# A two-layer streaming encoder: the sample's result turned in the value product's bank, and a rearranged start of layer A

## The chip, the cores and the metric

The kernel runs on one core of a Trainium2 chip. The metric is the device time of one execution in microseconds (us). Five engines work side by side, each through its own instruction list in order: TensorE (PE) multiplies and transposes, ScalarE (ACT) and VectorE (DVE) work on what PE leaves in its result banks, GpSimd (POOL) works on buffers, and SyncE (SP) issues every DMA transfer of this kernel. They wait for one another through semaphores.

## The reference: what is computed

Two layers, one after the other, over a prompt of 2048 tokens and a sample of 64 tokens that has caches of earlier keys and values. Cut to what matters:

```
def project(x, norm_g, w_in, q_g, k_g, n_heads, n_kv):
    h = rms_norm(x, norm_g)
    p = h @ w_in
...
    q, k, v, gate = jnp.split(p, [wq, wq + wkv, wq + 2 * wkv], axis=-1)
...
    q = rms_norm(q.reshape(*lead, n_heads, HEAD_DIM), q_g)
    k = rms_norm(k.reshape(*lead, n_kv, HEAD_DIM), k_g)
...
    op = prompt_band_attention(qp, kp, vp, past_chunks, bias_fn, sinks)
    y_p = x_p + (op * jax.nn.silu(gp)) @ w_out
...
    os_, nk, nv = sample_band_attention(qs, ks, vs, ck, cv, bias_fn, sinks)
    y_s = x_s + (os_ * jax.nn.silu(gs)) @ w_out
```

The model width is 1024, with 16 heads of 64. Layer A (index 0) has two key/value heads and a window of two earlier chunks of 64 tokens; layer B has 16 key/value heads and eight earlier chunks. The outputs are both results and the newest keys and values of both layers.

## The kernel before

**Precision.** Every fp32 operand is split into a high and a low part (`split_to`, line 579, and the casts in `load_act.split`): ScalarE casts the high part, DVE or POOL subtracts it from the source for the low part. A product is then three matmuls: high weight by high x, low weight by high x, high weight by low x (lines 477 to 479 in `project`).

**Units and passes.** The prompt is cut into eight units of 256 tokens (two tiles of 128); the sample is a ninth unit of 64. The order of the units is 0 to 6, the sample, 7. Layer A runs four passes `qd` over the units, each with four query heads; the first pass also projects k and v. Layer B runs eight passes `hp`, each with one pair of heads. At the end of a layer come output projections (`output_jobs`, lines 1366 to 1371).

**What sets the order.** PE's order is written out by hand: attention steps are emitted one by one, and `Filler` puts projection matmuls between them up to a mark. On the other engines a scheduler sets the order from the order of the code, the buffers and its own estimate of times. `Background` collects small steps (splits, low parts) and hands them out between attention steps; `behind` adds a dependency that only fixes an order on an engine.

**Result banks.** PE's results go to banks named by tags: `pj` (projections, two banks), `tp` (transpositions of queries, keys and gates, one bank), `o` (value products, one bank), and for scores and probabilities `sa` in layer A (four) or `sb` in layer B (two pairs). A step that takes a tag waits until the earlier user of that bank has been read.

**Layer B, one item.** For each unit of a head pair: `queries` transposes q and k into `tp`, ScalarE takes the high parts out (L1095, L1096) and DVE the low parts (L1100, L1104). `scores` multiplies (L1146, L1147), DVE adds the bias and takes the minimum (L1150), ScalarE takes the exponential (L1154), POOL forms the gate product G (L1168). `values` transposes the probabilities into `sb` (L609, five tiles at a time) and splits them into the tiles `ph` and `pl` (L581, L582), of which each has six slots for key tiles. `outputs` multiplies with the values in bank `o` (L1242, L1243). For the sample unit, `sample_outputs` multiplies in bank `o`, ScalarE and DVE add up the pieces (L1209, L1211), POOL multiplies by the gate (L1212), and `sample_turned` transposes this result into `tp`, from where ScalarE copies it out in two halves (L1219) for the store. The sample's turn occurs once in each head pair, eight times in all. As the sample unit is the last but one, the turn comes when `queries` for the next head pair's first unit has just filled `tp`.

**Bias tiles.** `bias_tile` loads the bias of a head into `BT` (L188) and POOL overwrites a corner (L189, L191). The bias vectors get to the form in which they are read over a copy: `spread` loads a row to all partitions (L170) and stores it skewed (L171). `spread_first` does it for the first four heads at once, through a tile that it borrows from `ph` (L197, L202).

**The start of layer A.** `load_act` loads x of a unit in four pieces into raw buffers `xraw` (L368; three buffers, `XB`), casts each (L382 on ScalarE, L383 on POOL) and, for the first two units, squares them (`square`). From the sums come the token scales (`token_scales`, `sums_to_scales`: two small matmuls L429, DVE, a power on POOL L434). For later units `row_scales` loads rows of x again into `xraw` (L451), ScalarE squares with a running sum (L453), POOL adds (L458) and raises to the power (L460). `first` projects unit 0, `gen` every other unit; `take_kv` and `take_qg` evacuate a projection, where ScalarE multiplies with the scale (L500). After unit 0, `first` also calls `token_scales` for unit 1.

Of the kernel before, what the change touches and what calls it, by code (L numbers as in the profile page):

```python
# [15 lines left out]
P = 128  # L16
# [5 lines left out]
UT = 256  # L22
# [11 lines left out]
XB = 3  # L34
# [16 lines left out]
def hybrid_encoder_kernel(  # L51
# [142 lines left out]
    def spread_first():  # L194
        row = t("ph", [P, 6, 256], 2, F32R).bitcast(F32).rearrange("p a b -> p (a b)")[:, : 4 * VL]
        src = vec[0, 0]
        ld = load(  # L197
            row.rearrange("p (h v) -> p h v", v=VL),
            bass.AP(tensor=src.tensor, offset=src.offset, ap=[[0, P], [VL, 4], [1, VL]]),
        )  # L200
        behind(ld.ins, held["w"])
        store(skew[0, 0:4].rearrange("h p v -> p h v"), row.rearrange("p (h v) -> p h v", v=VL))  # L202
        b = BT[:, 0:1024].rearrange("p (h k) -> p h k", h=4)
        src = skew[0, 0, 0, 127:128]
        load(b, bass.AP(tensor=src.tensor, offset=src.offset, ap=[[VL - 1, P], [P * VL, 4], [1, 256]]))
        nc.gpsimd.memset(b[0:64, :, 192:256], BIG)
        nc.gpsimd.memset(b[64:128, :, 0:64], BIG)
        return [b[:, h] for h in range(4)]
# [139 lines left out]
    def load_act(src, o, T, squares=False, joint=False, lead=None, cache=None, cached=False):  # L348
# [22 lines left out]
        def split(c):  # L371
            def fn():
                if len(raws) <= c:
                    bg.run(x.squares[c - XB])
                rv = raws[c]
                xx = t("xx", [P, 4 * OT], XN, F32R)
                xh, xl = parts = parts_of(xx, T, joint)
                if joint:
                    nc.scalar.copy(xh[:, :, :T], rv)
                    nc.gpsimd.tensor_tensor(xh[:, :, T:], rv, xh[:, :, :T].bitcast(F32), op=ALU.subtract)  # L380
                else:
                    nc.scalar.copy(xh, rv)  # L382
                    nc.gpsimd.tensor_tensor(xl, rv, xh.bitcast(F32), op=ALU.subtract)  # L383
                x.parts.append(parts)
                if cache is not None:
                    store(kept(c), xx[:, : 4 * T].bitcast(F32))
                if not squares:
                    fetch()
            return fn

        def square(c):
            def fn():
                s2 = t("res", [P, 2 * OT], 2)[:, : 2 * T].rearrange("p (k s) -> p k s", k=2)
                sq = nc.scalar.activation(s2, raws[c], AF.Square)
                if lead is not None and c > 0:
                    behind(sq.ins, held["wh"])
                part = t("o1" if x.sum else "G", [P, 256])
# [88 lines left out]
    def evacuate(layer, tt, n, ps, C, G, b=None):  # L486
# [11 lines left out]
        for dst, src in pieces:  # L498
            if n == P:
                nc.scalar.activation(dst, src, AF.Identity, scale=sc)  # L500
            else:
                nc.scalar.activation(dst[:n], src[n:], AF.Identity, scale=sc[n:])
# [173 lines left out]
    def layer_a():  # L676
# [4 lines left out]
        def add_unit(qd, place, unit):  # L681
# [59 lines left out]
            def first():  # L741
# [13 lines left out]
                for it, o in zip(mine, qgs):  # L755
                    take_qg(it, o[0])
                st.bias[0] = spread_first()
                token_scales(units[1], st.x[0, 1], psum("o", 512, 1))
                yield 2 * 3 * 512 / 2400

            def gen():
# [8 lines left out]
                for it in mine:  # L770
                    if qd == 0 and not heads_up:
                        out = []
                        c = yield from project(it.tile, xc, st.wkv, 256, out)
                        take_kv(it, out[0])
# [149 lines left out]
        def values(it):  # L924
            qd = it.qd
            tt, t0, n = it.tile
            ph = t("ph", [P, 6, 256], 2, F32R)
            pl = t("pl", [P, 6, 256], 2, F32R)
# [77 lines left out]
    def layer_b():  # L1006
# [168 lines left out]
        def values(it, i, h):  # L1175
            u, T, tiles = it.unit
            tt, t0, n = tiles[i]
            if i == 0:
                it.ph[h] = t("ph", [P, 6, 256], 2, F32R)
                it.pl[h] = t("pl", [P, 6, 256], 2, F32R)  # L1180
# [7 lines left out]
            for c in range(m):  # L1188
                transpose(PTv[:, c, :n], it.p[i, h][:n, c * P : (c + 1) * P])
            bg.anchor(*split_to(  # L1190
                it.ph[h][:, kb : kb + m, t0 : t0 + n], it.pl[h][:, kb : kb + m, t0 : t0 + n], PTv[:, :m, :n]
            ))
# [21 lines left out]
        def sample_turned(it):  # L1214
            tp = psum("tp", 512, 1)
# [7 lines left out]
        def outputs(it, h):  # L1223
# [15 lines left out]
            mm.append((VT[:, tb, h], tb - it.base, P, UT))  # L1239
# [272 lines left out]
```

## Time and profile before

| | us |
|---|---|
| median of three runs | 2322.2 |
| the three runs | 2326.36, 2320.93, 2322.2 |
| the profiled execution | 2330.51 |
| its span, first to last instruction | 2328.7 |
| PE busy in the span | 2259.3 |
| mean granted clock of PE | 0.991 |

A page of the profile gives the busy time of each engine, and groups of instructions by line. `L609` is line 609 of the kernel; where a helper records an operation, the line is the helper's (every transposition is L609), and the buffers tell what it is. `tp<-ident,o` is an instruction that writes `tp` and reads `ident` and `o`. In a timeline the first two columns are the start and the duration of an instruction, both in us; in brackets stands the idle time just ahead of it and what ended that. In a list of waits the columns are the total in us, the count and the longest. SPq is SP's list of DMA issues; the time there is that of the issue, not of the transfer. `DMA to landing` gives the time from issue to arrival for the transfers of one line.

### The profile page before, as it was taken

Reading aid. Unit: us, or ns where it says so; the run is one execution under the profiler, and the core shown is the slowest. Engines: PE = TensorE matmul, PEld = TensorE weight load, DVE = VectorE, ACT = ScalarE, POOL = GpSimd, SP = SyncE. Lnnn points to the kernel's source line nnn. Section 1 sums busy time; section 2 is a strip of 40 time slices with the busy share of each in tenths; the row PEclk is TensorE's granted clock in tenths of the full one; section 3 lists DMA queues with packets and bytes.
Section 4 is the critical chain, followed back from the end, with each engine's and each line's share of the span. In section 5 each row is a group of like instructions: output and inputs, shape, how many; then the busy total and the mean of one; then the engine's idle time right before and its main releaser. Section 6 shows DMA issues by size and latency. Waiting matters only on the chain.

```text
span 2328.7 us, 42202 instructions
## 1 busy us (share of the span) xinstructions
PE 2259.3 (97%) x13869; PEld 1984.3 (85%) x13869; DVE 1559.2 (67%) x5194; ACT 1432.8 (62%) x3632; POOL 839.5 (36%) x1196
## 2 busy tenths in 40 slices
PE   7899999999999999999999999999999999999999
PEld 6787888888889998888888888888888888888999
DVE  6779888887784446776767757667667577576211
ACT  6778877777773336765656656656556566565321
POOL 5554533333354556432222222222223222224443
PEclk9999999999999999999999999999999999999999
DMA  8846546754437767454543544544445435443665
GB/s 250 265 152 204 170 147 189 220 176 159 141 110 208 226 212 261 157 184 125 167 126 104 175 133 129 154 134 119 139 134 158 125 113 174 123 125 106 187 186 148
DMA packets 232124, 379.35 MB, mean 163 GB/s; under 512 B 24720, under 2 KB 163360, under 8 KB 231872
## 3 DMA queue, kind: packets, MB, share of 16 engines
q1 hardware_dynamic: 231904, 376.65, 52.7%
q8 instruction: 109, 1.79, 0.3%
q14 instruction: 111, 0.91, 0.1%
HBM read 296.13 MB, written 82.08 MB: 162 GB/s over the span
## 4 chain that ended last, share of the span: by engine, by line
PE 79%; DVE 8%; DMA 5%; ACT 4%; issue 2%; POOL 1%; SPq 1%; DVEq 0%; ACTq 0%; POOLq 0%
PE pj L477 13%; PE pj L479 12%; PE pj L478 12%; PE pj L1366 5%; PE pj L1367 5%; PE pj L1368 5%; PE sb L609 5%; PE o L1243 3%; PE o L1242 3%; PE tp L609 3%; PE sb L1147 3%; PE sb L1146 3%; DMA xraw<-in_x_rows_dram 2%; PE sa L609 2%; DVE pl L582 1%
## 5 line engine op out<-in xcount | busy, mean ns | idle before, releaser
L477 PE MATMUL pj<-wh,xx 128*128 128x512 f32 (+1 forms) x1648 | 671.0, 407 | 9.2 <-ACT pb L500 8.6
L479 PE MATMUL pj<-wh,xx 128*128 128x512 f32 (+1 forms) x1648 | 641.3, 389 | 0.0
L478 PE MATMUL pj<-wl,xx 128*128 128x512 f32 (+1 forms) x1648 | 638.7, 388 | 1.0 <-DVE wl L312 1.0
L479 PEld LDWEIGHTS pj<-wh,xx 128*128 128x128 f32 x1648 | 312.6, 190 | 68.3
L477 PEld LDWEIGHTS pj<-wh,xx 128*128 128x128 f32 x1648 | 314.1, 191 | 50.3 <-ACT pb L500 9.9
L478 PEld LDWEIGHTS pj<-wl,xx 128*128 128x128 f32 x1648 | 314.8, 191 | 40.0 <-DVE wl L312 1.4
L383 POOL TENSOR_TENSOR xx<-xraw,xx 128x528 fp32r<-128x528 f32 (+1 forms) x200 | 264.9, 1341 | 197.1 <-ACT xx L382 185.0
L540 POOL TENSOR_TENSOR f<-f,mhalf 128x4 f32<-128x4 f32 (+3 forms) x221 | 226.1, 1024 | 227.9 <-DVE f L536 219.0
L1154 ACT ACTIVATE p<-p,nm 128x640 f32<-128x640 f32 (+5 forms) x264 | 199.8, 757 | 175.2 <-DVE nm L1150 174.6
L1366 PE MATMUL pj<-xx,wh 128*128 128x264 f32 x1024 | 294.2, 287 | 1.2 <-DVE res L1371 1.0
L1367 PE MATMUL pj<-xx,wh 128*128 128x264 f32 x1024 | 291.7, 285 | 0.0
L1368 PE MATMUL pj<-xx,wl 128*128 128x264 f32 x1024 | 290.3, 283 | 0.0
L1150 DVE CUSTOM_DVE_ANT_0 p<-sb,BT 128x640 f32<-128x640 f32 (+5 forms) x272 | 196.8, 724 | 136.0 <-PE sb L1147 120.9
L582 DVE TENSOR_TENSOR pl<-sb,ph 128x640 fp32r<-128x640 f32 (+4 forms) x264 | 193.3, 732 | 117.0 <-ACT ph L581 114.2
L1002 POOL TENSOR_TENSOR o<-gt,o 128x256 f32<-128x256 f32 (+1 forms) x132 | 102.9, 779 | 386.1 <-DVE o L1001 122.8
L382 ACT CAST xx<-xraw 128x528 fp32r<-128x528 f32 (+1 forms) x200 | 122.2, 626 | 190.1 <-PE pj L1368 97.5
L581 ACT CAST ph<-sb 128x640 fp32r<-128x640 f32 (+4 forms) x264 | 163.5, 619 | 116.4 <-PE sb L609 111.1
L1366 PEld LDWEIGHTS pj<-xx,wh 128*128 128x128 f32 x1024 | 193.1, 189 | 2.1 <-DVE res L1371 1.6
L1367 PEld LDWEIGHTS pj<-xx,wh 128*128 128x128 f32 x1024 | 192.9, 188 | 0.2
L1368 PEld LDWEIGHTS pj<-xx,wl 128*128 128x128 f32 x1024 | 193.1, 189 | 0.0
L536 DVE CUSTOM_DVE_ANT_0 sq<-pa 128x64 f32<-128x64 f32 (+1 forms) x834 | 169.6, 256 | 30.8 <-ACT pa L500 28.8
L1371 DVE TENSOR_TENSOR res<-pj,res 128x264 f32<-128x264 f32 x128 | 55.0, 430 | 200.2 <-PE pj L1368 184.9
(210 smaller groups left out, 4788.6 us busy)
## 6 DMA issues: line engine op xcount, KB each, us to landing
xx<-xsb SPq DMA_DIRECT2D x224, 512.0 KB, 4.3
xx<-xsa SPq DMA_DIRECT2D x88, 512.0 KB, 4.8
xraw<-oga SPq DMA_DIRECT2D x64, 264.0 KB, 3.6
xraw<-ogb SPq DMA_DIRECT2D x64, 264.0 KB, 3.3
xsa<-xx SPq DMA_DIRECT2D x32, 512.0 KB, 4.5
wraw<-in_w_in_b_dram SPq DMA_DIRECT2D x64, 256.0 KB, 3.7
xsb<-xx SPq DMA_DIRECT2D x32, 512.0 KB, 4.0
xraw<-in_x_dram SPq DMA_DIRECT2D x40, 256.0 KB, 4.1
```

The source lines that it names most:

```text
L383: nc.gpsimd.tensor_tensor(xl, rv, xh.bitcast(F32), op=ALU.subtract)
L477: nc.tensor.matmul(ps[:n, :C], xh, wh, start=k == 0, stop=False)
L478: nc.tensor.matmul(ps[:n, :C], xh, wl, start=False, stop=False)
L479: nc.tensor.matmul(ps[:n, :C], xl, wh, start=False, stop=k == KC - 1)
L540: nc.gpsimd.tensor_tensor(fv, fv, mhalf[:n, :H], op=ALU.pow)
L582: b = nc.vector.tensor_tensor(dst_lo, src, dst_hi.bitcast(F32), op=ALU.subtract)
L609: nc.tensor.transpose(out, in_, ident[:n, :n])
L1150: mi = nc.vector.tensor_tensor_reduce(out=p[r, :nk], in0=S[r, o : o + nk], in1=b, op0=ALU.add, op1=ALU.min, scale=1.0, scalar=3e38, accum_ ...
L1154: ex = nc.scalar.activation(p[:n, :nk], p[:n, :nk], AF.Exp, scale=-1.0, bias=it.nm[:n, c : c + 1], accum_out=it.sm[:n, c : c + 1],)
L1366: nc.tensor.matmul(ps[:, :OT], wh, oh, start=k == 0, stop=False)
L1367: nc.tensor.matmul(ps[:, :OT], wh, ol, start=False, stop=False)
L1368: nc.tensor.matmul(ps[:, :OT], wl, oh, start=False, stop=k == KC - 1)
```

## The change

1. `sample_turned` takes bank `o` in place of `tp`.
2. There are four raw buffers for x in place of three (`XB`).
3. The tiles `ph` and `pl` have five key slots in place of six; in layer B the slot of a key tile is its index modulo five.
4. `spread_first` works in two halves of two heads each, since the borrowed tile is smaller: two loads and two stores in place of one each.
5. The casts of the third unit (the first without squares) are put behind the last square, and its second to fourth also behind the last evacuation of unit 0.
6. The token scales of unit 1 are computed in `gen` of unit 1, after its first k/v projection, and not at the end of `first`.

```
-XB = 3
+XB = 4
...
     def spread_first():
-        row = t("ph", [P, 6, 256], 2, F32R).bitcast(F32).rearrange("p a b -> p (a b)")[:, : 4 * VL]
...
-        store(skew[0, 0:4].rearrange("h p v -> p h v"), row.rearrange("p (h v) -> p h v", v=VL))
+        for h in (0, 2):
+            row = t("ph", [P, 5, 256], 2, F32R).bitcast(F32).rearrange("p a b -> p (a b)")
+            row = row[:, : 2 * VL].rearrange("p (h v) -> p h v", v=VL)
+            src = vec[0, h]
+            ld = load(row, bass.AP(tensor=src.tensor, offset=src.offset, ap=[[0, P], [VL, 2], [1, VL]]))
+            behind(ld.ins, held["w"])
+            store(skew[0, h : h + 2].rearrange("h p v -> p h v"), row)
...
+                if not squares and "first" in held:
+                    behind(cast.ins, held["square"])
+                    if c:
+                        behind(cast.ins, held["first"])
+                    if c == 3:
+                        held.pop("first")
...
+                held["square"] = sq.ins
...
-                nc.scalar.activation(dst, src, AF.Identity, scale=sc)
+                held["evac"] = nc.scalar.activation(dst, src, AF.Identity, scale=sc).ins
...
+                held["first"] = held["evac"]
                 st.bias[0] = spread_first()
-                token_scales(units[1], st.x[0, 1], psum("o", 512, 1))
...
                         c = yield from project(it.tile, xc, st.wkv, 256, out)
+                        if u == 1 and it is mine[0]:
+                            token_scales(unit, xc, psum("o", 512, 1))
                         take_kv(it, out[0])
...
-                transpose(PTv[:, c, :n], it.p[i, h][:n, c * P : (c + 1) * P])
+                transpose(PTv[:, (kb + c) % 5, :n], it.p[i, h][:n, c * P : (c + 1) * P])
...
         def sample_turned(it):
-            tp = psum("tp", 512, 1)
+            tp = psum("o", 512, 1)
             transpose(tp[0:HD, 0:P], it.o)
...
-            mm.append((VT[:, tb, h], tb - it.base, P, UT))
+            mm.append((VT[:, tb, h], (tb - it.base) % 5, P, UT))
```

Line numbers in the changed kernel are six to eight higher. The counts of instructions are the same on every engine, but for one load and one store more on SP. Three places of the order follow; a row gives the line, the operation and what it writes and reads.

PE at the second sample turn in layer B, before. `pj` is the projection of the next pass, `p` the probabilities, `o` in the fourth row the sample's result.

```order
L478 MATMUL pj_15645<-wl_14665,xx_15437 128x512
L479 MATMUL pj_15645<-wh_14664,xx_15437 128x512
L609 MATMUL sb_15652<-ident,p_15560 128x128 x5
L609 MATMUL tp_15666<-ident,o_3141_15590 64x128
L477 MATMUL pj_15645<-wh_14670,xx_15439 128x512
L478 MATMUL pj_15645<-wl_14671,xx_15439 128x512
```

The same place on PE after the change:

```order
L484 MATMUL pj_15648<-wl_14668,xx_15440 128x512
L485 MATMUL pj_15648<-wh_14667,xx_15440 128x512
L615 MATMUL sb_15655<-ident,p_15563 128x128 x5
L615 MATMUL o_15669<-ident,o_3142_15593 64x128
L483 MATMUL pj_15648<-wh_14673,xx_15442 128x512
L484 MATMUL pj_15648<-wl_14674,xx_15442 128x512
```

The turn keeps its place; only its bank is another, `o` for `tp`.

ACT in the head before, from the first k/v evacuation of unit 1 (`pa_545<-pj_520`). `res_481` is the first row scale, `KA`, `KB` and `VT` are keys and values.

```order
L500 ACTIVATE pa_545<-pj_520,rms_92 128x256
L816 ACTIVATE KA<-sa_559,ksc 64x128
L816 ACTIVATE KB<-sa_559,ksc 64x128
L560 CAST VT<-pa_545 128x2x64
L850 ACTIVATE q_133_574<-tp_571,qsc 64x2x128 x2
L500 ACTIVATE pa_596<-pj_555,rms_92 128x256
L500 ACTIVATE pb_597<-pj_555,rms_92 128x256
L453 ACTIVATE res_481,ms_478<-xraw_479 128x512
```

ACT there after the change, up to the same evacuation, now `pa_548<-pj_517`. The eight L459 are the row scales of units 2 and 3, the three L587 the casts of the cached keys and values.

```order
L459 ACTIVATE res_478,ms_475<-xraw_476 128x512
L459 ACTIVATE res_482,ms_475<-xraw_480 128x512
L459 ACTIVATE res_486,ms_475<-xraw_484 128x512
L459 ACTIVATE res_490,ms_475<-xraw_488 128x512
L459 ACTIVATE res_499,ms_496<-xraw_497 128x512
L459 ACTIVATE res_503,ms_496<-xraw_501 128x512
L459 ACTIVATE res_507,ms_496<-xraw_505 128x512
L459 ACTIVATE res_511,ms_496<-xraw_509 128x512
L587 CAST KSA<-res_665 64x128
L587 CAST KSB<-res_665 64x128
L587 CAST VS<-res_665 128x2x64
L506 ACTIVATE pa_548<-pj_517,rms_92 128x256
```

The evacuation stood ahead of every row scale and stands behind all eight now.

POOL in the head before, around the token scale of unit 1 (`rms_92<-ms_451`). The L383 are the low parts of x, the L540 powers of the head norms.

```order
L383 TENSOR_TENSOR xx_466<-xraw_456,xx_466 128x512
L540 TENSOR_TENSOR f_417<-f_417,mhalf 128x4
L434 TENSOR_TENSOR rms_92<-ms_451,mhalf 128x2
L540 TENSOR_TENSOR f_432<-f_432,mhalf 128x4
L383 TENSOR_TENSOR xx_470<-xraw_458,xx_470 128x512
L540 TENSOR_TENSOR f_550<-f_550,mhalf 128x2
```

POOL after the change, around the same scale, now `rms_92<-ms_545`. The L464 and L466 belong to the row scales, the memsets to bias tiles.

```order
L464 TENSOR_TENSOR ms_492<-ms_475 128x2
L189 MEMSET BT 64x64
L191 MEMSET BT 64x64
L466 TENSOR_TENSOR rms_92<-ms_492,mhalf 128x2
L189 MEMSET BT 64x64
L191 MEMSET BT 64x64
L464 TENSOR_TENSOR ms_513<-ms_496 128x2
L466 TENSOR_TENSOR rms_92<-ms_513,mhalf 128x2
L440 TENSOR_TENSOR rms_92<-ms_545,mhalf 128x2
L546 TENSOR_TENSOR f_553<-f_553,mhalf 128x2
```

The scale of unit 1 stood ahead of the row scales' steps and stands behind the last of them now.

More of the change, by code (lines that the diff above doesn't have):

```diff
@@ L194, in spread_first @@
     def spread_first():
-        row = t("ph", [P, 6, 256], 2, F32R).bitcast(F32).rearrange("p a b -> p (a b)")[:, : 4 * VL]
[L196 to L201, printed above, removed]
-        store(skew[0, 0:4].rearrange("h p v -> p h v"), row.rearrange("p (h v) -> p h v", v=VL))
+        for h in (0, 2):
[5 more added lines that the diff above has]
+            store(skew[0, h : h + 2].rearrange("h p v -> p h v"), row)
         b = BT[:, 0:1024].rearrange("p (h k) -> p h k", h=4)
@@ L378, in fn @@
                 if joint:
-                    nc.scalar.copy(xh[:, :, :T], rv)
+                    cast = nc.scalar.copy(xh[:, :, :T], rv)
                     nc.gpsimd.tensor_tensor(xh[:, :, T:], rv, xh[:, :, :T].bitcast(F32), op=ALU.subtract)
                 else:
-                    nc.scalar.copy(xh, rv)
+                    cast = nc.scalar.copy(xh, rv)
                     nc.gpsimd.tensor_tensor(xl, rv, xh.bitcast(F32), op=ALU.subtract)
+                if not squares and "first" in held:
[4 more added lines that the diff above has]
+                        held.pop("first")
                 x.parts.append(parts)
@@ L926, in values @@
             tt, t0, n = it.tile
-            ph = t("ph", [P, 6, 256], 2, F32R)
-            pl = t("pl", [P, 6, 256], 2, F32R)
+            ph = t("ph", [P, 5, 256], 2, F32R)
+            pl = t("pl", [P, 5, 256], 2, F32R)
             hi, lo = [], []
@@ L1178, in values @@
             if i == 0:
-                it.ph[h] = t("ph", [P, 6, 256], 2, F32R)
-                it.pl[h] = t("pl", [P, 6, 256], 2, F32R)
+                it.ph[h] = t("ph", [P, 5, 256], 2, F32R)
+                it.pl[h] = t("pl", [P, 5, 256], 2, F32R)
             if u == NU:
@@ L1188, in values @@
             for c in range(m):
-                transpose(PTv[:, c, :n], it.p[i, h][:n, c * P : (c + 1) * P])
-            bg.anchor(*split_to(
-                it.ph[h][:, kb : kb + m, t0 : t0 + n], it.pl[h][:, kb : kb + m, t0 : t0 + n], PTv[:, :m, :n]
-            ))
+                transpose(PTv[:, (kb + c) % 5, :n], it.p[i, h][:n, c * P : (c + 1) * P])
+            bg.anchor(*split_to(it.ph[h][:, :m, t0 : t0 + n], it.pl[h][:, :m, t0 : t0 + n], PTv[:, :m, :n]))
         def then(it, i, h):
```

## The prediction

> **What bounds the kernel now.** The page comes first, then the list of what TensorE (PE) waited for.
>
> ```profile
> PE 2259.3 (97%) x13869; PEld 1984.3 (85%) x13869; DVE 1559.2 (67%) x5194; ACT 1432.8 (62%) x3632; POOL 839.5 (36%) x1196
> ```
> ```profile
> PE tp L609 <- DVE KB L1104: 21.7, 7, 3.4
> PE pj L477 <- ACT pb L500: 8.6, 5, 3.2
> ```
>
> PE is busy 97% of the span, and the change takes no matmul away, so it can act only on PE's idle time and on PE's clock. The largest wait is one line that occurs seven times: the transposition of the sample's result waits until VectorE (DVE) has made the low part of the next head pair's keys. Both use the one bank `tp`; its reader stands late in DVE's queue. So I read PE's timeline next, at the first of these turns, at the second and at the seventh. Each fence holds the transposition of probabilities ahead of the turn, the turn, and the transposition of probabilities two later.
>
> ```profile
> 1038.15 0.71 PE L609 MATMUL sb<-ident,p 128*128 128x128 f32 x5
> 1040.56 0.27 PE L609 MATMUL tp<-ident,o 128*64 128x128 f32 x1 [1.70 <-DVE KB L1104]
> ...
> 1049.02 0.71 PE L609 MATMUL sb<-ident,p 128*128 128x128 f32 x5
> ```
> ```profile
> 1195.17 0.71 PE L609 MATMUL sb<-ident,p 128*128 128x128 f32 x5
> 1199.23 0.40 PE L609 MATMUL tp<-ident,o 128*64 128x128 f32 x1 [3.34 <-DVE KB L1104]
> ...
> 1199.85 0.63 PE L478 MATMUL pj<-wl,xx 128*128 128x512 f32 x1
> ...
> 1204.75 0.40 PE L478 MATMUL pj<-wl,xx 128*128 128x512 f32 x1
> ...
> 1210.16 0.71 PE L609 MATMUL sb<-ident,p 128*128 128x128 f32 x5
> ```
> ```profile
> 1993.19 0.71 PE L609 MATMUL sb<-ident,p 128*128 128x128 f32 x5
> 1997.22 0.40 PE L609 MATMUL tp<-ident,o 128*64 128x128 f32 x1 [3.33 <-DVE KB L1104]
> ...
> 2006.94 0.71 PE L609 MATMUL sb<-ident,p 128*128 128x128 f32 x5
> ```
>
> A wait of 1.70 us leaves the clock alone: the turn itself takes 0.27 us. A wait of 3.3 us is followed by slow matmuls: 512 columns take 0.63 us from 1199.85 on, and 0.40 again from 1204.75. So a turn costs more than its idle time. That is the first term.
>
> **Term 1: the turn in bank `o`.** The first stretch is 1049.02 − 1038.15 = 10.87 us, of which 1.70 waits; without it the same matmuls take 9.17. The second is 1210.16 − 1195.17 = 14.99, the seventh 13.75. The six long ones (second to seventh) sum to 87.08. Six unstalled ones would be 6 × 9.17 = 55.02, which leaves 32.06; with the 1.70 of the first the removable time is 33.8 us. The eighth turn does not wait. About 20.0 of it (6 × 3.34) is idle time, 12.0 is slow clock.
>
> [...]
>
> Is anything late next? In the new bank the turn needs four things: its input from GpSimd (POOL), bank `o` read by ScalarE and DVE (their sum is POOL's input, so that is earlier), bank `o` returned by ScalarE's two copies before the next value product, and the scores' and probabilities' buffers behind it.
>
> ```profile
> 1193.61 0.14 POOL L189 MEMSET BT<- 64x64 f32 x1 [4.22 <-DMA BT<-skew]
> 1193.72 0.33 POOL L1212 TENSOR_TENSOR o<-G,o 128x64 f32<-128x64 f32 x1
> ```
> ```profile
> 1197.25 0.82 DVE L582 TENSOR_TENSOR pl<-sb,ph 128x640 fp32r<-128x640 f32 x1
> 1198.59 0.49 DVE L1104 SCALAR_TENSOR_TENSOR KB<-tp,ksc,KB 64x256 fp32r<-64x256 f32 x1
> 1199.31 0.29 DVE L554 SCALAR_TENSOR_TENSOR pb<-sq,pb 128x128 f32<-128x128 f32 x1
> ```
> ```profile
> 1197.11 0.31 ACT L553 ACTIVATE sq<-pb 128x128 f32<-128x128 f32 x1
> ```
> ```profile
> 1205.69 0.36 PE L1242 MATMUL o<-ph,VT 128*128 128x256 f32 x1
> ```
> ```profile
> 1514.57 0.32 POOL L1212 TENSOR_TENSOR o<-G,o 128x64 f32<-128x64 f32 x1
> ```
> ```profile
> 1515.15 0.71 PE L609 MATMUL sb<-ident,p 128*128 128x128 f32 x5
> ```
>
> What PE waits for now is DVE's step at 1198.59; the new bank has no such reader. POOL has the input at 1194.05 and PE would be there after 1195.17 plus its five transpositions, about 1195.8: no wait. The tightest turn is the fourth: ready at 1514.89, PE there about 1515.76, so 0.9 us to spare. ScalarE is free of the step ahead of its two copies at 1197.4 (1197.11 + 0.31), so these would be done about 1197.9. The value product at 1205.69 comes to about 1199.8, when 3.34 idle, the slow stretch and the matmuls between are kept or dropped as above: 1.9 us to spare. The next scores' minimum on DVE follows L554, so about 1199.6, and PE needs their exponentials only at 1210.16 less 5.8, some 1204.4: covered by the projection matmuls between. On ScalarE the `ph` cast of the next value product now stands ahead of the exponential of those scores; both fit before 1204.4 as well, with some 2 us left. If that cover is gone, each turn loses what is missing. One new wait can be named: in POOL's order the second bias tile's memset (it waits for a DMA) moved ahead of the gate product L1168 of the next unit. Bound: 0 to about 1 us a head pair, 7 in all; taken at 0, since PE needs that product only after the transposition that stands at 1210.16. A gain beyond 33.8 is excluded here, since nothing else is taken off PE.
>
> **Term 2: the head.** Three edits act on the first 65 us: the third unit's casts are held back, the second unit's scale is put after its first k/v projection, and four raw buffers rotate. PE first:
>
> ```profile
> 34.19 0.58 PE L477 MATMUL pj<-wh,xx 128*128 128x256 f32 x1 [3.18 <-ACT pb L500]
> ...
> 38.57 0.39 PE L477 MATMUL pj<-wh,xx 128*128 128x512 f32 x1
> ...
> 44.45 0.29 PE L477 MATMUL pj<-wh,xx 128*128 128x256 f32 x1
> ```
> ```profile
> 29.73 0.47 ACT L500 ACTIVATE pa<-o,rms 128x256 f32<-128x256 f32 x1 [1.64 <-POOL rms L434]
> ...
> 32.78 0.62 ACT L382 CAST xx<-xraw 128x512 fp32r<-128x512 f32 x1 [1.83 <-DMA xraw<-in_x_dram]
> ...
> 39.63 0.47 ACT L500 ACTIVATE pa<-pj,rms 128x256 f32<-128x256 f32 x1 [2.10 <-PE sa L609]
> ...
> 45.75 0.63 ACT L453 ACTIVATE res<-xraw 128x512 f32<-128x512 f32 x1 [0.26 <-DMA xraw<-in_x_rows_dram]
> ...
> 63.36 0.62 ACT L453 ACTIVATE res<-xraw 128x512 f32<-128x512 f32 x1
> ```
>
> The gain comes first. ScalarE's cast at 32.78 waits 1.83 us for a load and stands ahead of the evacuations that PE waits for; held behind them, it lets PE start about 32.2 instead of 34.19: −2.0.
>
> The cost is in the order. Before, the second unit's first k/v is evacuated at 39.63 and the eight row scales (L453) are spread from 45.75 to 63.36, between evacuations. Now all eight, and three cache casts, stand ahead of that evacuation on ScalarE, and its scale on POOL stands behind the eight too. `pj` has two banks: PE can run the k/v (4.4 us, to 36.6) and the q/gate projection (38.57 to 44.45 is 5.9, to 42.5), and then its next projection, the one of 44.45, must wait for the evacuation. So PE waits for the eighth row load. On SyncE's queue that load stands behind two pairs of bias rows and their stores.
>
> ```profile
> 25.35 0.59 SPq L197 DMA_DIRECT2D ph<-vec  x1
> ...
> 34.95 1.60 SPq L170 DMA_DIRECT2D row<-vec  x2
> ```
> ```profile
> DMA to landing us min/median/max: 3.9/5.6/6.9
> ```
> ```profile
> DMA to landing us min/median/max: 4.0/5.2/7.1
> ```
> ```profile
> DMA to landing us min/median/max: 3.2/4.6/8.1
> ```
> ```profile
> 64.96 0.69 POOL L460 TENSOR_TENSOR rms<-ms,mhalf 128x2 f32<-128x2 f32 x1
> ```
>
> The three tails are of L170 (row load), L171 (its store) and L451 (raw row load). In the new order the first pair of row loads stands right behind the loads that took L197's place, so between 25.35 and 34.95; I take 29 (estimate). Two rounds of row load and store follow: 29 + 5.6 + 5.2 + 5.6 + 5.2 = 50.6; with the issues between about 52.5. The eighth load lands 5 later, 57.6. Its scale (0.8 with the read of the sum), the casts beside it, the two powers on POOL (0.69 each) and the evacuation (0.47) bring PE to about 61.1: 16.6 after 44.45. A wait of that length drops the clock: +2.0 as in term 1. On the other side, waits that PE has behind this place fall away or shrink, since the other engines catch up while it stands. Those are, first for 44 to 120 us, then for 120 to 235:
>
> ```profile
> PE pj L477 <- ACT pb L500: 3.9, 2, 2.3
> PE o L947 <- DVE pl L582: 2.6, 2, 1.5
> ```
> ```profile
> PE tp L609 <- DVE pa L545: 2.1, 2, 1.8
> ```
>
> They are 8.6 us; I take 5. Term 2 is 16.6 + 2.0 − 5 ≈ +13 (the −2.0 moves PE's arrival, not the end of this wait, so it is not counted). Lower bound, all loads at the fastest: 29 + 2 × (3.9 + 4.0) + 3.2 + 3.5 = 51.5 and 1 for issues, 8.0 after 44.45, + 2 − 8.6: about 1, say 0. Upper bound, all at the slowest: 29 + 2 × (6.9 + 7.1) + 8.1 + 3.5 = 68.6, 24.1 after 44.45, + 2, little given back: +25.
>
> **Term 3: the rest, 0.** The probability tiles have five key slots in place of six, indexed round; transpositions, casts and subtractions keep count and shape, so their times stay. The split of the first bias spread moves the same bytes with one load and one store more on SyncE, beside PE's first projections; uncovered, 0.6 us an issue (25.35). The fourth buffer also lets the output projections' loads run further ahead, but no output-projection wait for x stands in PE's list. These two hold within a microsecond or two either way.
>
> **Sum.** The profiled execution took 2330.51 us (span 2328.7), 8.3 above the median of 2322.2; I apply the terms to the median: 2322.2 − 33.8 + 13 + 0 ≈ 2301, own range 2289 (head 0) to 2313 (head +25).
>
> **The rivals.** *The head is covered* (18%): the rows land early or ScalarE is not held long; for it speak L451's 3.2, against it the two rounds of bias rows on the queue. 2322.2 − 33.8 = 2288. *The head costs its upper bound* (10%): 2313. *The turn only moves PE's work onto a backlog* (9%): with PE 5 us earlier, the minimum and exponential of the next scores are late and half the gain goes; for it speak the three DVE steps up to 1199.6, against it the 4.8 us until PE needs them. 2322.2 − 17 + 13 = 2318. *The turn waits as long in bank `o`* (9%), the one on the slower side: the transposition's input stands on POOL behind the bias tile's memset L189, which waited 4.22 us for its DMA at 1193.61. If that load lands late, PE waits for POOL instead of DVE. The point from which it decides is 0.9 us of slack plus some 2.2 us of wait, 3.1 later than now, for most turns; then term 1 is gone and the head alone is left: 2322.2 + 13 = 2335. Against it: at the two turns shown POOL was ready 1.7 and 0.9 us ahead of PE.
>
> **How the numbers follow.** The forecast has 54%. The range 2286 to 2318 takes in the covered head, the head's upper bound and the backlog, and leaves out the fourth rival and tails beyond the bounds. About 0.2% (4.6 us) is what a measurement of this kernel tells from no change: faster means below 2317.6, slower above 2326.8. Faster: 54 + 18 + 10 + 2 of the backlog's 9 = 84%; same 7%; slower 9%.
>
> **What would show it.** Right: in PE's list of waits the line `tp` L609 behind DVE's KB is gone, the turns' stretches are 9.2 to 9.5 us, and no wait of the turn for POOL's product has taken its place. In the head, PE's third projection for `pj` starts about 61 with a wait of 15 to 20 us on ScalarE's evacuation, behind eight row scales in a row. Wrong: a wait of the turn on POOL, of the value product on ScalarE's copies, or of the next transposition on the exponential, of over 1 us each; or PE without a wait over 5 us between 40 and 65 us.

## The result and the profile after

| | before | after |
|---|---|---|
| median of four runs, first measurement | 2322.47 us | 2304.75 us (runs 2303.25 to 2307.44) |
| ratio, with its 95% interval | | 0.9922 (0.9905 to 0.994) |
| median, measured again beside other runs | 2327.21 us | 2302.64 us |
| ratio, with its 95% interval | | 0.9897 (0.9882 to 0.9911) |
| span of the profiled execution | 2328.7 us | 2302.8 us |

The change is faster by 17.7 us in the first measurement and by 24.6 in the second; the intervals overlap. Of the 6.9 us between the two, 4.7 are of the kernel before, whose four runs in the first measurement have a lower median than the nine in the second. The forecast was 21 us faster, 2301 us.

The page of the changed kernel and its list of PE's waits (total in us, count, longest):

```profile
PE 2247.6 (98%) x13869; PEld 1978.6 (86%) x13869; DVE 1572.6 (68%) x5194; ACT 1429.2 (62%) x3632; POOL 843.5 (37%) x1196
```
```profile
PE pj L483 <- ACT pa L506: 19.7, 1, 19.7
PE o L483 <- ACT wh L308: 5.8, 1, 5.8
PE sb L615 <- DVE pl L588: 4.1, 8, 0.6
```

The line that led the list before, 21.7 us of the turn, is gone. In its place stands one single wait of 19.7 us for an evacuation. (The second row is the first projection's, 6.3 us before; its weight cast stands on L309 there, since lines ahead of the casts moved up by one.) Both are what the prediction had looked for. PE's timeline at the second and at the seventh turn:

```profile
1202.49 0.71 PE L615 MATMUL sb<-ident,p 128*128 128x128 f32 x5
1203.03 0.27 PE L615 MATMUL o<-ident,o 128*64 128x128 f32 x1
...
1211.45 0.71 PE L615 MATMUL sb<-ident,p 128*128 128x128 f32 x5
```
```profile
1972.13 0.71 PE L615 MATMUL sb<-ident,p 128*128 128x128 f32 x5
1972.67 0.27 PE L615 MATMUL o<-ident,o 128*64 128x128 f32 x1
...
1981.10 0.71 PE L615 MATMUL sb<-ident,p 128*128 128x128 f32 x5
```

The turn has no bracket, so PE does not wait, and the stretches are 8.96 and 8.97 us (before: 14.99 and 13.75). POOL, the engine that the slower rival rested on, at the second turn:

```profile
1201.48 0.14 POOL L189 MEMSET BT<- 64x64 f32 x1 [4.76 <-DMA BT<-skew]
1201.60 0.32 POOL L1218 TENSOR_TENSOR o<-G,o 128x64 f32<-128x64 f32 x1
...
1210.06 0.14 POOL L189 MEMSET BT<- 64x64 f32 x1 [5.72 <-DMA BT<-skew]
1210.18 0.76 POOL L1176 TENSOR_TENSOR G<-pb,sm 128x128 f32<-128x128 f32 x2
```

The input is ready at 1201.92 (1201.60 + 0.32), 1.1 us ahead of the turn at 1203.03. Over the seven turns it is 1.1 to 1.7 us ahead; at the fourth, which was taken for the tightest, 1.2. The second memset does wait 5.72 us with the gate product behind it, as the new order said, but PE shows no wait for it.

In the head, PE, ScalarE and POOL of the changed kernel:

```profile
30.70 0.39 PE L483 MATMUL pj<-wh,xx 128*128 128x256 f32 x1 [0.49 <-ACT pb L506]
...
59.90 0.58 PE L483 MATMUL pj<-wh,xx 128*128 128x256 f32 x1 [19.72 <-ACT pa L506]
```
```profile
41.64 0.63 ACT L459 ACTIVATE res<-xraw 128x512 f32<-128x512 f32 x1 [3.92 <-DMA xraw<-in_x_rows_dram]
...
56.34 0.63 ACT L459 ACTIVATE res<-xraw 128x512 f32<-128x512 f32 x1 [1.46 <-DMA xraw<-in_x_rows_dram]
...
58.52 0.30 ACT L587 CAST KSA<-res 64x128 fp32r<-64x128 f32 x1 [1.46 <-DMA res<-in_ckt_a_dram]
...
59.37 0.84 ACT L506 ACTIVATE pa<-pj,rms 128x256 f32<-128x256 f32 x2
```
```profile
57.68 0.69 POOL L466 TENSOR_TENSOR rms<-ms,mhalf 128x2 f32<-128x2 f32 x1 [0.28 <-DVE ms L465]
58.34 0.70 POOL L440 TENSOR_TENSOR rms<-ms,mhalf 128x2 f32<-128x2 f32 x1
```

The chain is the forecast one: eight row scales, each behind its DMA, from 41.64 to 56.34, the cache casts, then the evacuation. One wait in it was not forecast: the cache casts stand 1.46 us for their own load, beside the two powers on POOL, which end at 59.04. PE goes on at 59.90 (forecast 61.1).

PE's order is nearly the same in all kernels of this document, so the start of the same matmul can be compared between two traces. That gives a table by stage: how much later (+) or earlier (−) than in the first trace of before PE reaches the matmul that started there at the time in the heading. All but the first row are runs of the next section.

| trace | 86 us | 208 us | 649 us | 1009 us | 2053 us | 2293 us |
|---|---|---|---|---|---|---|
| the change | +14.8 | +2.7 | +2.9 | +9.1 | −25.8 | −25.9 |
| the change, again | +14.3 | +2.5 | +4.9 | +6.7 | −28.0 | −28.1 |
| before, again | −1.7 | −3.8 | −4.0 | −4.0 | −7.5 | −9.1 |
| turn alone in `o` | −1.2 | −3.4 | −1.5 | −2.0 | −37.0 | −37.1 |
| all but the turn | +15.0 | +2.8 | +3.7 | +7.1 | +7.2 | +7.2 |
| scale back in `first` | −2.2 | −10.8 | −11.7 | −8.9 | −43.6 | −43.6 |
| that, three raw buffers | −2.7 | −3.2 | −2.6 | −3.6 | −38.7 | −39.1 |
| that (four), casts free | −4.9 | −14.2 | −13.0 | −9.0 | −43.7 | −43.7 |
| rows behind the evacuation | −2.7 | −13.9 | −12.8 | −7.2 | −41.9 | −42.0 |
| three fetched ahead | −5.4 | −15.6 | −14.2 | −9.9 | −44.6 | −44.5 |
| raw buffers alone | −4.3 | −15.6 | −13.4 | −11.3 | −13.3 | −14.7 |

The seven turns that waited lie between 1009 and 2053 us: the change gains 34.9 us there (+9.1 to −25.8). The stall shows as +14.8 at 86 us and is mostly paid back by 208 us. A further loss, 6.2 us in the first trace and 1.8 in the second, stands between 649 and 1009 us, at the end of layer A and the start of layer B.

### The profile page after: what moved, and what is told of

It reads as the page before. It is cut to its first block, busy times and chain, and to the rows that moved or that the text cites. A ratio compares the mean times of both kernels' runs of the same rounds, so it can differ in the third digit from the quotient of the medians.

```text
span 2302.8 us, 42224 instructions
## 1 busy us (share of the span) xinstructions
PE 2247.6 (98%) x13869; PEld 1978.6 (86%) x13869; DVE 1572.6 (68%) x5194; ACT 1429.2 (62%) x3632; POOL 843.5 (37%) x1196
## 4 chain that ended last, share of the span: by engine, by line
PE 83%; DVE 6%; ACT 4%; DMA 3%; issue 2%; POOL 1%; SPq 1%; ACTq 0%; POOLq 0%; DVEq 0%
PE pj L483 14%; PE pj L485 13%; PE pj L484 13%; PE pj L1372 5%; PE sb L615 5%; PE pj L1373 5%; PE pj L1374 5%; PE o L1249 3%; PE tp L615 3%; PE o L1248 3%; PE sb L1155 3%; PE sb L1154 2%; PE sa L615 2%; PE sa L901 1%; PE sa L902 1%
## 5 line engine op out<-in xcount | busy, mean ns | idle before, releaser
L483 PE MATMUL pj<-wh,xx 128*128 128x512 f32 (+1 forms) x1648 | 667.6, 405 | 20.3 <-ACT pa L506 19.7
L587 ACT CAST ph<-sb 128x640 fp32r<-128x640 f32 (+4 forms) x264 | 163.4, 619 | 124.6 <-PE sb L615 119.8
L918 ACT ACTIVATE p<-p,nm 128x257 f32<-128x257 f32 (+2 forms) x272 | 134.5, 497 | 79.1 <-DVE nm L912 67.7
```

What stands on the lines that cost most here:

```text
L483: nc.tensor.matmul(ps[:n, :C], xh, wh, start=k == 0, stop=False)
```

## The experiments

Ratios are to the kernel before on the same chip, with 95% intervals.

**The turn alone** in bank `o`:

```
         def sample_turned(it):
-            tp = psum("tp", 512, 1)
+            tp = psum("o", 512, 1)
```

> The kernel before with one edit: the sample's turn takes bank o. Prediction's theory: the seven waits of the turn go with their slow clock and nothing takes their place, -33.8 us, so 2322.5 - 33.8 = 2288.7, ratio about 0.9855. Rival A (the turns are worth only what the whole change gained beyond its small loss up to 240 us, 17.7 + 2.7 = 20.4, the rest being peculiar to the one profiled execution of before): about 2302. Rival B (a wait for the new bank comes up): over 2310, with a wait for bank o in PE's list. The head stays as before: no wait over 5 us on PE between 40 and 65 us, offset at 240 us within 1 us of before.

Measured: 2293.49 us beside 2326.91, ratio 0.9863 (0.9849 to 0.9876), 33.4 us faster. PE's list of waits starts so:

```profile
PE o L947 <- DVE pl L582: 6.8, 10, 1.5
PE o L477 <- ACT wh L309: 6.0, 1, 6.0
PE pj L477 <- ACT pb L500: 5.3, 4, 2.9
```

No line is of the turn. The two for bank `o` are of layer A (L947) and of the first projection, and before had them with 6.9 and 6.3 us. Term 1 stands with its size, and both rivals fall. The unstalled stretches are 0.2 us shorter than the prediction took them: 8.95 to 8.98 us here and 8.96 to 8.98 in the change, where 9.17 stood and 9.2 to 9.5 were named as the sign.

**All but the turn**: the change with that one line turned back.

> The whole change, but the turn in bank tp as before. Prediction's term 2 (head +13 net): 2322.5 + 13 = 2335.5, ratio about 1.0056. Rival (the stall at 40 to 60 us is given back by 240 us, as the two traces show, +2.7): 2325, ratio about 1.001. If the four raw buffers cost the further 6.3 us by which the changed kernel's trace falls back between 640 and 1040 us: about 2331. The turns wait 3.3 us each again, 21 to 22 us in all.

Measured: 2335.6 us beside 2326.91, ratio 1.0044 (1.0031 to 1.0058), 8.7 us slower. That lies between the two theories: more than what the stall leaves at 208 us (+2.8 in the table), less than 13. Another 3.4 us go between 649 and 1009 us (+3.7 to +7.1). The two parts add up: −33.4 + 8.7 = −24.7, and the whole change measured again gives −24.6.

**The scale back in `first`**: the change, but the second unit's token scale is called where it was.

```
                 st.bias[0] = spread_first()
+                token_scales(units[1], st.x[0, 1], psum("o", 512, 1))
...
-                        if u == 1 and it is mine[0]:
-                            token_scales(unit, xc, psum("o", 512, 1))
```

> The whole change, but the second unit's token scale is called at the end of the first unit again. Its order on ACT then has the evacuation of the second unit's first k/v ahead of all row scales. Both theories: PE's wait of 19.7 us is gone. Prediction's term 2: the stall costs 13 net, so about 2304.75 - 13 = 2292. Rival (nearly all of the stall is given back behind it): 3 us or less, about 2302, with waits for probabilities and evacuations of about 10 us back between 60 and 235 us.

Measured: 2287.3 us beside 2326.91, ratio 0.9837 (0.9822 to 0.9852), 39.6 us faster than before. The stretch of the stall in this kernel, and in the change (PE, PEld, DVE, ACT and POOL busy, clock, DMA share, GB/s):

```profile
42.00:62.00 20.00, 20.00 (x127) 17.80 (x127) 15.27 (x65) 17.27 (x53) 9.73 (x22) 1.00 0.93 300
```
```profile
42.00:62.00 20.00, 2.10 (x10) 2.11 (x11) 3.19 (x20) 8.12 (x25) 5.54 (x16) 0.52 0.75 239
```

PE works through, where the change lets it stand for 18 of 20 us. Against the change measured again (2302.64) the stall costs 15.3 us by medians, 15.0 when each is taken against the kernel before on its own chip, for a wait of 18 to 20: PE reaches it some microseconds early, its slow clock (0.52 over these 20 us) comes on top, and 3.5 us are given back (in the table the two kernels are 17.0 apart at 86 us, 13.5 at 208). The prediction's 13 for the stall holds; the rival that nearly all is given back falls. So this version is faster than both kernels.

**Before, again**, unchanged, for a second trace.

> The kernel before, unchanged, for a second trace. If the 8 us by which its profiled execution (2330.5) stands over the median are peculiar to that execution, this one is within 3 us of 2322.5 and its PE timeline is shorter at some places: if by shorter slow stretches behind the turns, the six long stretches sum to less than 87.08 us by some 8; if elsewhere, they sum to 87 again and the turns are worth 33.8 in every execution. Timed against itself: ratio 1.000 within its interval.

Measured: 2326.07 us beside 2326.91, ratio 0.9996 (0.9985 to 1.0008); the profiled span is 2319.7 us, 9.0 shorter than in the first trace. The table says where: 3.8 us in the first 208 us, 3.5 at the turns, 1.6 behind 2053 us. So part of the answer is each. The six long stretches sum to 83.48 us here (14.04, 12.46, 14.02, 15.17, 13.77, 14.02), not 87.08. One of them, the third turn in this trace:

```profile
1350.17 0.71 PE L609 MATMUL sb<-ident,p 128*128 128x128 f32 x5
1354.20 0.27 PE L609 MATMUL tp<-ident,o 128*64 128x128 f32 x1 [3.33 <-DVE KB L1104]
...
1362.63 0.71 PE L609 MATMUL sb<-ident,p 128*128 128x128 f32 x5
```

It waits 3.33 us as all the others do, and the turn takes 0.27 us: 12.46 − 3.33 = 9.13, no slow clock at all. What a wait costs beyond itself varies from turn to turn and from run to run, in these six from 0 to 2.7 us (15.17 − 3.33 − 9.13).

**The change, again**, beside the next three.

> The changed kernel, unchanged, beside the next three on one chip. If the parts add up as the turn alone (2293.49 against 2326.91) and the rest alone (2335.6 against 2326.91) say, it is 33.4 - 8.7 = 24.7 us below the kernel before, ratio about 0.989; if they do not add up, the ratio stays at 0.992 (17.7 us) as first measured. The trace shows PE's wait of 17 to 20 us near 40 to 60 us again.

Measured: 2302.64 us beside 2327.21, ratio 0.9897 (0.9882 to 0.9911). The parts add up. PE waits 18.1 us for the evacuation again.

**Three raw buffers** and **free casts**: the version with the scale back in `first`, once with `XB = 3`, once with four buffers and without the five lines that hold back the third unit's casts.

```
-XB = 4
+XB = 3
```
```
-                if not squares and "first" in held:
-                    behind(cast.ins, held["square"])
-                    if c:
-                        behind(cast.ins, held["first"])
-                    if c == 3:
-                        held.pop("first")
```

> The version with the second unit's scale back at the end of the first unit (39.6 us below before), with three raw buffers in place of four. Theory (the four buffers let row loads and x run ahead, and this is most of the 6 us that the start gained beside the stall): 5 to 8 us slower than that version, ratio to before about 0.986, with evacuation and probability waits of PE of some 10 us between 44 and 235 us. Rival (the held casts gave it): within 3 us of that version, ratio 0.984.

> The same version (scale at the end of the first unit, four raw buffers), without the holding back of the third unit's casts. Theory (the four buffers gave the start's gain): within 3 us of that version, ratio 0.984, though PE's wait of about 3 us for an evacuation near 30 to 34 us comes back. Rival (the held casts gave it): 5 to 8 us slower, ratio 0.986 to 0.987.

Measured: three buffers 2292.19 us, ratio 0.9853 (0.9836 to 0.9869); casts free 2286.35 us, ratio 0.9828 (0.9814 to 0.9842), both beside 2327.21. Against 2287.3 and 2286.35 the fourth buffer is worth 4.9 to 5.8 us by medians (the ratios' intervals overlap, but no run with three is below 2291.17, and none with four, casts free, above 2287.46); the held casts are worth nothing that can be measured beside four buffers. The version with three buffers still has the five-slot tiles, the spread in halves and the held casts. It is 35.0 us below before, 1.6 more than the turn alone, so these edits together are worth little. PE between 45 and 120 us, with three and with four, casts free:

```profile
45.00:120.00 75.00, 68.62 (x408) 57.74 (x408) 53.60 (x198) 59.34 (x173) 40.45 (x63) 1.00 0.80 255
```
```profile
45.00:120.00 75.00, 73.23 (x446) 63.12 (x445) 61.07 (x220) 64.17 (x188) 44.07 (x70) 1.00 0.83 266
```

PE is busy 4.6 us more of these 75. With the casts held as well (scale back in `first`) it is 3.1 us more. By 208 us the four buffers are 7.6 us ahead with the casts held (−3.2 against −10.8) and 11 with them free (−14.2), by 1009 us 5.3 and 5.4. The wait for an evacuation near 30 us, expected back without the held casts, did not come back. PE waits there for a weight's low part, without the held casts and with them:

```profile
PE pj L478 <- DVE wl L311: 2.9, 1, 2.9
```
```profile
PE pj L484 <- DVE wl L311: 3.0, 1, 3.0
```

With the casts held and three buffers, the wait for the evacuation is there, but short:

```profile
PE pj L483 <- ACT pb L506: 0.9, 1, 0.9
```

The turn alone, with neither edit, still has it with 2.9 us. So this wait is small or gone with held casts or with a fourth buffer, and the held casts gain nothing beside the fourth buffer.

**Row scales behind the evacuation**: the change with the scale where it puts it, but `row_scales` of units 2 and 3 written behind unit 1's first `take_kv`.

```
-                    for later in order[place + (place > 2) : place + 2]:
-                        row_scales(later)
+                    late = order[place + (place > 2) : place + 2]
+                    if place == 2:
+                        st.rows = late
+                    else:
+                        for later in late:
+                            row_scales(later)
...
                         take_kv(it, out[0])
+                        if u == 1 and it is mine[0]:
+                            for later in st.rows:
+                                row_scales(later)
                         yield c
```

> The whole change with the scale where the change puts it, but the row scales of units 2 and 3 are written behind the second unit's first evacuation; ACT has that evacuation ahead of all eight then, POOL the second unit's scale ahead of theirs. Theory (the stall comes from the eight row scales standing ahead of the evacuation, wherever the scale is computed): no wait over 5 us near 40 to 60 us and about 15 us faster than the changed kernel, ratio to before about 0.984. Rival (the late place of the scale itself makes PE wait): a wait of over 5 us stays, and less than 8 us are gained.

Measured: 2288.47 us beside 2327.21, ratio 0.9836 (0.982 to 0.9852), 14.2 us faster than the change beside it. Between 30 and 70 us PE has one wait left:

```profile
PE pj L483 <- ACT pb L506: 0.2, 1, 0.2
```

The stall is gone with the scale in its late place. What made it is that the row scales stood ahead of the evacuation, not where the scale is computed in itself.

**Lows early**: the kernel before, turn in `tp`, but DVE makes the low parts of the next head pair in one go.

```
                         queries(its[x + 1])
+                        if x and its[x - 1].unit[0] == NU:
+                            for q in its[x + 1].todo:
+                                bg.run(q)
```

> The kernel before, turn still in tp, but DVE makes both halves of the next head pair's low parts in one go, ahead of the probabilities' split that stands between them before. By before's trace DVE is then done with tp at about 1197.9 instead of 1199.08, so the turn's wait shrinks from 3.34 to about 2.1 us. Theory (the idle time and the slow clock behind it are two costs, and the clock needs more than about 2 us of idle time): idle 7 x 1.2 = 8 us less and most of the 12 us of slow clock gone, 15 to 20 us faster, ratio 0.992 to 0.9935. Rival A (any wait of over 1 us slows the clock): 8 us, ratio 0.9965. Rival B (the bank is not what PE waits for): no change of the waits.

Measured: 2311.69 us beside 2324.17, ratio 0.9943 (0.993 to 0.9956), 12.5 us faster. The waits shrank less than worked out, to 2.6 us:

```profile
PE tp L609 <- DVE KB L1104: 17.3, 7, 2.6
```
```profile
1188.52 0.71 PE L609 MATMUL sb<-ident,p 128*128 128x128 f32 x5
1191.84 0.27 PE L609 MATMUL tp<-ident,o 128*64 128x128 f32 x1 [2.62 <-DVE KB L1104]
...
1200.27 0.71 PE L609 MATMUL sb<-ident,p 128*128 128x128 f32 x5
```
```profile
1501.88 0.71 PE L609 MATMUL sb<-ident,p 128*128 128x128 f32 x5
1505.21 0.40 PE L609 MATMUL tp<-ident,o 128*64 128x128 f32 x1 [2.62 <-DVE KB L1104]
...
1514.96 0.71 PE L609 MATMUL sb<-ident,p 128*128 128x128 f32 x5
```

The first stretch is 11.75 = 9.13 + 2.62: a wait of 2.6 us and no slow clock. Five of the six are like it (11.73 to 11.77); the fourth turn, the last fence, has 13.08, of which 1.34 is slow clock. Idle time fell only 4.4 us (21.7 to 17.3), and the kernel gained 12.5. So idle time and slow clock are two costs, and waits that are 0.7 us shorter took most of the second with them here (five of six turns have none). The rival that any wait of over 1 us slows the clock falls, and so does the one that the bank is not what PE waits for. The size expected, 15 to 20, was not reached: the wait fell to 2.6 and not to 2.1, and 4.4 us of idle time went in place of 8.

**Three fetched ahead in the output projections**: the version with free casts, where `load_act` fetches three ahead there and four elsewhere.

```
-        for _ in range(XB):
+        for _ in range(ahead):
...
-                st.x[j] = x = load_act(og[layer], o, OT)
+                st.x[j] = x = load_act(og[layer], o, OT, ahead=3)
```

> The version with the scale at the end of the first unit and without held casts (2286.35 beside a before of 2327.21), where the output projections fetch only three raw buffers ahead, the rest four. Theory (the fourth buffer gains about 10.7 us up to 200 us and costs about 5 us in the output projections and the start of layer B, as the traces with three and four buffers show): about 2281, ratio 0.9805, and PE's wait of 1.9 us for DVE's sum near 690 us shrinks below 1. Rival (that loss is chance, by the place of a slow stretch): within 2 us of 2286.

Measured: 2287.52 us beside 2324.17, ratio 0.9839 (0.9826 to 0.9853): no gain on 2286.35. The wait that was to shrink is as long as with four, in this kernel between 660 and 900 us:

```profile
PE pj L1365 <- DVE res L1370: 2.6, 3, 1.9
```

The theory that the look-ahead of the output projections costs the 5 us falls; but it is not chance either, since every trace with four buffers loses 1.8 to 6.2 us between 649 and 1009 us (the table), and those with three lose nothing.

**Raw buffers alone**: the kernel before with four raw buffers, five-slot tiles and the spread in halves (the version with free casts, with the turn back in `tp`).

> The kernel before with four raw buffers, five-slot probability tiles and the spread in halves alone (turn in tp, scale at the end of the first unit, casts free). Theory (the parts add up): 40.9 - 33.4 = 7.5 us faster than before at most, 4 to 8, ratio 0.997 to 0.998. Rival (the gain of four buffers hangs on the turn's bank): within 2 us of before.

Measured: 2319.72 us beside 2324.17, ratio 0.9977 (0.9965 to 0.9989), 4.5 us faster, as the sum of the parts says.

## Why the prediction was right, point by point

**Term 1, −33.8.** Right in mechanism and size: the turn alone gives −33.4. The new bank brought no wait, and the slack that was worked out held. What the prediction did not see is that the 12 us of slow clock in it are not fixed: in the second trace of before the same six stretches hold 28.5 us of waits and slow clock (83.48 − 55.02) in place of 32.06, of which 20.0 are waits in both.

Waits of 3.33 us are followed here by 0 to 2.7 us of slow clock (the stretches less 9.17 and the wait), waits of 2.6 us by 1.3 in one case of six and by none in five. A wait of 1.93 us elsewhere (below) was followed by it too. So here the length alone did not decide.

The granted clock shows more. Behind the turns it is 0.50 for 3.41 us or for 6.83 us, and in one trace these slow spells begin whole multiples of 3.413 us apart (in the first trace of before at 1197.92, 1358.35, 1518.78, 1679.20, 1836.21 and 1996.64 us, in the second at 1195.28, 1512.72, 1669.73, 1830.16 and 1990.59 us). Cut the time at these multiples into slices of 3.41 us, and each wait falls into one or two of them. Five traces have the turn in `tp`: before twice, all but the turn, raw buffers alone, lows early; they hold 35 waits. Behind all 24 that leave 2.01 us or more of one slice idle stands slow clock, behind none of the 11 that leave 1.92 or less. Here are the slices of two waits, the third turn of the second trace of before and the fourth of lows early (span, its length, then busy time of PE, PEld, DVE, ACT, POOL, clock, DMA share, GB/s):

```profile
1348.88:1352.29 3.41, 1.99 (x12) 1.44 (x10) 3.25 (x15) 3.35 (x9) 1.97 (x4) 1.00 0.79 270
1352.29:1355.71 3.42, 1.50 (x8) 1.27 (x9) 2.23 (x5) 0.55 (x3) 0.00 (x0) 1.00 0.02 5
```
```profile
1501.31:1504.73 3.42, 1.27 (x9) 0.85 (x7) 3.30 (x16) 2.77 (x7) 1.71 (x3) 1.00 0.57 208
1504.73:1508.14 3.41, 2.93 (x8) 2.38 (x9) 1.78 (x4) 0.43 (x2) 0.00 (x0) 0.50 0.04 10
```

The first wait has 3.33 us and leaves 1.42 and 1.92 us of its slices idle; no slow clock follows. The second has only 2.62 us, but 2.15 of them lie in one slice, and the next has a clock of 0.50. So in these five traces the slow clock went with the idle time that a wait left in one slice, not with the wait's length, and the slice was not idle as a whole: PE is busy 1.27 us in it. The bound of about 2 us is of these turns: the version that fetches three ahead has slow clock behind a slice with 1.44 us of idle time (672.67 to 676.08 us).

**Term 2, +13.** The chain was right: PE reached the stall at 40.2 (59.90 − 19.72; forecast 42.5), the eighth row load was issued at 52.47 (forecast 52.5) and PE left the stall at 59.90 (forecast 61.1). The stall alone costs 15.3 by medians, 14.2 by the rows behind the evacuation, 13.5 by the table at 208 us. Given back are 3.5 us of it, where 5 were taken. (The prediction's terms 16.6 + 2.0 − 5 make 13.6.)

**Term 3, 0.** This is the term that was mis-sized. The fourth raw buffer was taken at nothing; it is worth 4.5 (raw buffers alone) to 5.8 us: 8 to 11 gained up to 208 us, part of it lost again by 1009 us. The prediction put the buffers' work under the stall and looked at the output projections only, where PE did not wait for x; it did not ask what PE's short waits between 44 and 235 us (8.6 us in its three rows, 12.4 in all) were waiting for. With three buffers and no stall these waits are 11.4 us, with four and held casts 5.4. In the version with free casts, which has no stall, the waits of that stretch are these:

```profile
PE tp L609 <- ACT wh L308: 2.1, 1, 2.1
PE o L948 <- DVE pl L582: 2.0, 4, 0.7
PE tp L609 <- DVE pa L545: 0.2, 1, 0.2
```

So most of what the prediction set against the stall was the buffers' gain: behind 86 us the change makes up 12.1 us (+14.8 to +2.7), but the version without the stall makes up 8.6 as well (−2.2 to −10.8), and only 3.5 are left for engines that catch up while PE stands.

**The sum.** −33.4 (turn), +15.3 (stall), −5.4 (buffers, middle of the two) and 0 (casts) are −23.5, beside −24.6 and −17.7 measured. The forecast's −20.8 missed the buffers' −5.4, took the stall 2.3 too small and the turn 0.4 too large. Terms 2 and 3 together have a run of their own: all but the turn is +8.7, where +13 was forecast. That the forecast came within 4 us of both measurements is therefore in part luck: two errors of opposite sign stand in it.

**What stays open.** Why the kernels with four raw buffers lose 1.8 to 6.2 us between 649 and 1009 us. Two pieces are seen. One is a wait for DVE (last section). The other is the clock behind it, in the first trace of the change:

```profile
691.23 0.51 PE L1372 MATMUL pj<-xx,wh 128*128 128x264 f32 x1 [1.93 <-DVE res L1377]
```
```profile
683.00:718.00 35.00, 32.91 (x236) 31.23 (x234) 23.89 (x54) 18.69 (x48) 13.59 (x19) 0.90 0.48 151
```

The granted clock is 0.90 over these 35 us, which is 3.4 us of slow clock. The clock makes much of the difference between the traces. From 660 to 720 us it is 1.00 in the three that lose least (the change again 1.8, raw buffers alone 2.1, scale back in `first` 2.8). It is 0.97, some 1.7 us of slow clock, in the four that lose 3.4 to 5.6, and 0.94 in the first trace of the change, which loses 6.2. Without the slow clock 1.7 to 3.9 us remain. About 1 us of that is the wait for DVE; what the rest is, no run shows.

## What to carry to other kernels

A wait behind a single bank cost its length here and, where it left about 2 us of one slice of 3.41 us idle, up to 2.7 us more in slow clock (3.4 behind the wait of 1.93 us); shortening such waits a little can pay more than the idle time says (12.5 us for 4.4 of idle time in the version with the lows early). When an edit moves a small step (here a scale of two columns) behind others in the code, look where it lands on each engine's queue: one evacuation behind eight loads stopped the bottleneck engine for 20 us. Price every part of a change by the short waits it could remove, not only by the long ones it makes.

## What the runs showed of the hardware

A copy on DVE took 4.74 us here beside subtractions of POOL, 0.29 in the median of its line. In the kernel with free casts, DVE and POOL near 665 us:

```profile
664.98 5.05 DVE L863 CAST q<-q 64x256 fp32r<-64x256 f32 x2
```
```profile
665.44 3.88 POOL L382 TENSOR_TENSOR xx<-xraw,xx 128x528 fp32r<-128x528 f32 x3
```

and in the version with three raw buffers:

```profile
675.35 3.79 DVE L869 CAST q<-q 64x256 fp32r<-64x256 f32 x2
```
```profile
675.81 2.63 POOL L382 TENSOR_TENSOR xx<-xraw,xx 128x528 fp32r<-128x528 f32 x2
```

Two copies that take 0.29 us each in the median of their line take 5.05 us beside three subtractions of POOL, 3.79 beside two. In both, the first of the two is the long one (4.74 and 3.49 us), and it ends 0.4 us behind the last subtraction. With four buffers a third subtraction is ready at once (in the version that fetches three ahead too); this is the row of the copies' line (count, then shortest, median and longest in ns), with free casts, and the wait of PE for DVE's sum behind the copies, with three buffers:

```profile
L863 DVE CAST q<-q x136: 221/290/4743, 41.8 to 669.7; 64x256 fp32r<-64x256 f32 x128, 64x128 fp32r<-64x128 f32 x8
```
```profile
PE pj L1371 <- DVE res L1376: 0.9, 1, 0.9
```

With four buffers the longest of these waits is 1.9 us (the row of the version that fetches three ahead). Why the copies are long there, no run shows, and not every copy beside POOL is long: with free casts 45 of the line's 136 overlap a step of POOL and still take no more than 0.6 us. PE's wait is 1 us longer with four buffers than with three, and that is 1 us of the loss that stays open.
